# Row indices spread ahead of the gates' softmax, evictions between one-hots, keys and last modulation blocks by the Pool queue, four more blocks preloaded

## The chip, the cores and the metric

One core of one Trainium2 chip runs the whole kernel. The metric is the device time of one execution in microseconds (us); lower is better. The engines are TensorE (PE, with its weight loads PEld), VectorE (DVE), ScalarE (ACT), GpSimd (POOL) and SyncE (SP). Each works through its own queue in order. A DMA is issued from the queue of SP, ACT or POOL, and lands later.

## What is computed

One layer of a decoder for 256 tokens of width 1024: a token mixer, then PEER, a layer that picks for each token 128 of 16384 one-neuron experts. The change lies in PEER and in the modulation that its result is scaled by:

```python
mod = cs @ w_ada[l] + b_ada[l]              # six columns; the last, gt_f, scales PEER's result
q = (xt @ w_q).reshape(n, 8, 2, 128)
s = einsum('nhpd,phkd->nhpk', q, sub_keys)  # scores against two key tables of 128 per head
s1, i1 = top_k(s[:, :, 0], 16)
s2, i2 = top_k(s[:, :, 1], 16)
comb = s1[..., :, None] + s2[..., None, :]  # 256 candidates
top_s, pos = top_k(comb, 16)
experts = cand[pos]                         # cand = i1 * 128 + i2
gate = softmax(top_s)
a = gelu(einsum('nd,nhkd->nhk', xt, u_tab[experts]))
y = einsum('nhk,nhkd->nd', gate * a, v_tab[experts])
x = rmsnorm(x + gt_f * y)
```

## The kernel before

**Stages.** The mixer runs until about 274 us. Then come the queries (PE tile pq): 16 blocks of w_pq, each split by ACT (L98, tile hi) and DVE (L99, tile lo) into two parts, three products of eight matmuls each. `query` scales a block on DVE (L1174) and adds a bias on ACT (L1177). Between them stand the scores of token half 1 (`score`, PE tile psc) against the table `keys`, which SP loads at L1190. Then PEER's tables follow, dense: 128 blocks of `u` (PE tile pu, 16 instructions per block; "the u half"), ACT's gelu into the array W (`gelu`, every second block), and 128 blocks of `v` (PE tile Y, "the Y half"), which contract W. W lies in the tile GB, block by block. A table block is 512 KB; `table_ahead` (L746 to L754) issues it into a ring of ten tiles (tags raw and hl), from SP, one in five from ACT.

**Two ways for the tokens.** The last 96 tokens (SPARSE = 64 and 32) are not in the dense products (DT = 160 columns). For them POOL gathers the rows of the chosen experts by an indirect DMA of 128 rows of 4 KB, 512 KB (L1055): 96 gathers from u, 96 from v. DVE multiplies each u row with the token (L1076, a sum per row) and adds each v row, scaled, into `hrow` (L1085, L1087). The generator `sparse` holds four buffers and keeps three gathers ahead. Its indices come from the array `pairs`, which `spread` (L1036) writes from `own`, the indices and gates of token half 1, by six small DMAs from POOL. At the end PE folds hrow into Y (L1280) and the last sums, transposes and the output follow.

**From scores to one-hots.** `topk(tt)` runs on DVE for half 1, then for half 0: rounds of max, index and replace over eight heads, the combination, and the selection `sel` (L1004). Then it subtracts the maximum (L1008), ACT applies Exp (L1009), DVE normalises (L1012 to L1015), writes `own` (L1018, L1020), calls `spread`, and PE transposes indices and gates (tile pidx). `g_phase` works on chunks of 8 of the 160 dense tokens. Per chunk: DVE makes the one-hot `oe` (L1119) and scales it by the gate's high part `gth` into ob[:, 0] (L1121); ACT makes `od` with 8 instructions (L1125) and `oa` (L1129), and scales oe by the low part `gtl` into ob[:, 1] with 8 instructions (L1131); PE multiplies oa and ob (tile pG, 16 matmuls); and the result is evicted into W, by DVE for the blocks that already have their gelu (L1111, `kd` of 128) and by ACT for the others (L1113). Y needs all of W.

**What sets the order.** From the queries on the program order is written out. In the loop over u blocks `spend(work, more)` takes from the generators topk and g_phase as much as a budget allows: each `yield` names its cost, a block brings BU = 2.1. Once `n_first` is set, `due` grows by RATE = 0.75 per block, and each whole unit emits one gather product of `sparse` (and the gather that reuses its buffer) and takes 1.27 from the budget. In the Y half it is one per block. `ada_col(5)` sums the eight blocks of the last modulation column on DVE (L165): four in the stage before the queries, four among them (L1192), loaded by SP into the same four raw buffers as w_pq.

The lines that set the pace in the u half:

```python
        more = BU
        if n_first[0]:
            due[0] += RATE
            while due[0] >= 1:
                due[0] -= 1
                advance(rows)
                more -= 1.27
        if n_gated[0] and k % 2:
            more -= 0.45
        spend(work, more)
```

## Time and profile before

| | |
|---|---|
| time, three runs | median 980.07 us (977.72 to 986.09) |
| the profiled execution | 983.35 us, its span 981.6 us |
| PE | 919.2 us busy, 94% |
| DVE, ACT, POOL | 628.6, 356.3, 205.5 us busy |
| mean granted PE clock | 0.959 of full speed |
| DMA | 306.43 MB, 312 GB/s in the mean |
| queues | SP (q1) 179.39 MB, POOL (q0) 100.77 MB, ACT (q10) 25.17 MB |

The profile is one execution. In rows of windows the columns are: the stretch, its length, the busy time of PE, PEld, DVE, ACT and POOL (with the count of instructions), then PEclk, the granted clock as a share of 2.4 GHz (0.50 is 1.2 GHz), the busy share of the DMA engines and GB/s. A wait is put down to what ended it. Matmuls are pipelined: each fp32 matmul is two instructions here, and the pace is read from one start to the next.

### The profile page before, as it was taken

The page shows a single profiled execution, that of the slowest core. Times are in us where ns is not written, and L with a number is a line of the kernel's source. Part 1 is how long each engine was busy: PE and PEld are TensorE (multiplying, and loading weights), DVE is VectorE, ACT ScalarE, POOL GpSimd, SP SyncE. Part 2 cuts the span into 40 slices and gives each one's busy share as a digit, 9 for nine tenths or more (in the row PEclk, how much of TensorE's full clock was granted, in tenths as well). Part 3 has the DMA queues.
Part 4 walks back from the last instruction along what each step waited for, and adds up shares of the span by engine and source line. Part 5 has one row for each costly group of instructions (what it writes and reads, how often), then busy time and mean ns, then how long its engine had stood idle before and what let it go on. Part 6 is the DMA issues. An engine that isn't in the chain of part 4 may idle for free.

```text
span 981.6 us, 17461 instructions
## 1 busy us (share of the span) xinstructions
PE 919.2 (94%) x6794; PEld 886.5 (90%) x6794; DVE 628.6 (64%) x1373; ACT 356.3 (36%) x856; POOL 205.5 (21%) x212
## 2 busy tenths in 40 slices
PE   6999999999997999999979999989999999999926
PEld 5899887789987999999978999989999999999925
DVE  7898748866986791678875777654444444444463
ACT  4474348755545422101159998920000000000002
POOL 1000000000000001333433324333333333333340
PEclk8999869999997999999989999999999999999967
DMA  9888434356676487999998999979999999999981
GB/s 355 318 274 259 149 117 162 108 172 215 205 234 248 158 295 226 385 418 419 419 387 319 352 358 354 356 303 419 418 419 419 418 419 418 418 420 418 416 279 44
DMA packets 85810, 306.43 MB, mean 312 GB/s; under 512 B 9601, under 2 KB 10049, under 8 KB 85601
## 3 DMA queue, kind: packets, MB, share of 16 engines
q1 hardware_dynamic: 50976, 179.39, 49.4%
q0 software_dynamic: 27840, 100.77, 26.3%
q10 hardware_dynamic: 6912, 25.17, 6.7%
q8 instruction: 53, 0.87, 0.4%
q14 instruction: 29, 0.23, 0.1%
HBM read 304.14 MB, written 1.05 MB: 311 GB/s over the span
## 4 chain that ended last, share of the span: by engine, by line
PE 41%; DMA 33%; DVE 9%; issue 7%; ACT 6%; POOL 3%; DVEq 0%; ACTq 0%; POOLq 0%; SPq 0%
DMA gat<-in_v_row_dram,pairs 22%; PE pu L117 11%; DMA gat<-in_u_row_dram,pairs 8%; PE col L117 8%; PE pq L117 4%; POOL gat L1055 3%; DVE hrow L1087 3%; PE row L117 3%; PE pbr L117 2%; ACT od L1125 2%; ACT ob L1131 2%; PE po L117 2%; PE pout L117 1%; PE pS L117 1%; PE ph L117 1%
## 5 line engine op out<-in xcount | busy, mean ns | idle before, releaser
L117 PE MATMUL pu<-h,tab 128*128 128x160 f32 x2048 | 289.7, 302 | 5.4 <-ACT gb L1160 5.4
L117 PEld LDWEIGHTS pu<-h,tab 128*128 128x128 f32 x2048 | 283.3, 192 | 5.7 <-ACT gb L1160 5.7
L117 PE MATMUL Y<-gb,tab 128*128 128x160 f32 x2048 | 282.7, 300 | 1.3 <-DMA tab<-in_v_row_dram 0.8
L117 PEld LDWEIGHTS Y<-gb,tab 128*128 128x128 f32 x2048 | 279.8, 191 | 2.8 <-DMA tab<-in_v_row_dram 2.7
L1087 DVE SCALAR_TENSOR_TENSOR hrow<-gat,act,hrow 128x1024 f32<-128x1024 f32 x94 | 120.8, 1285 | 132.9 <-DMA gat<-in_v_row_dram,pairs 132.9
L1076 DVE SCALAR_TENSOR_TENSOR gat<-gat,hrow 128x1024 f32<-128x1024 f32 x96 | 116.4, 1221 | 53.1 <-DMA gat<-in_u_row_dram,pairs 52.5
L1055 POOL DMA_INDIRECT gat<-in_u_row_dram,pairs x96 | 105.1, 1095 | 195.4 <-DVE gat L1076 149.0
L1055 POOL DMA_INDIRECT gat<-in_v_row_dram,pairs x96 | 92.1, 959 | 171.7 <-DVE hrow L1087 149.1
L99 DVE TENSOR_TENSOR lo<-raw,hi 128x1024 fp32r<-128x1024 f32 (+2 forms) x67 | 80.5, 1207 | 24.5 <-ACT hi L98 24.1
L1302 ACT ACTIVATE gb<-gb 128x256 f32<-128x256 f32 x8 | 3.3, 417 | 224.2 <-DVE gb L1300 224.2
L98 ACT CAST hi<-raw 128x1024 fp32r<-128x1024 f32 (+2 forms) x67 | 69.1, 1038 | 43.1 <-PE pq L117 8.8
L1160 ACT ACTIVATE gb<-pu 128x320 f32<-128x320 f32 (+18 forms) x60 | 22.8, 382 | 114.7 <-PE pu L117 105.7
L165 DVE SCALAR_TENSOR_TENSOR raw<-raw,crow 128x1024 f32<-128x1024 f32 x48 | 58.2, 1220 | 9.8 <-DMA raw<-in_ada_t_dram 9.7
L1125 ACT ACTIVATE od<-iota,n1T 128x128 f16<-128x128 f16 x160 | 49.7, 439 | 0.0
L1131 ACT ACTIVATE ob<-oe,gtl 128x128 f16<-128x128 f16 x160 | 49.5, 429 | 0.0
L1111 DVE SCALAR_TENSOR_TENSOR gb<-pG,gb 128x480 f32<-128x480 f32 (+18 forms) x40 | 20.7, 557 | 38.5 <-PE pG L117 29.8
L117 PE MATMUL col<-hlo,hi 128*128 128x256 f32 x160 | 40.8, 289 | 0.0
L117 PE MATMUL col<-hh,hi 128*128 128x256 f32 x160 | 40.3, 286 | 0.0
L117 PE MATMUL pq<-hx,hi 128*128 128x258 f32 x128 | 33.4, 301 | 1.9 <-ACT gb L1176 1.9
L117 PE MATMUL col<-xr,wf 128*128 128x256 f32 x128 | 30.5, 404 | 4.3 <-ACT xr L271 4.3
L117 PEld LDWEIGHTS col<-xr,wf 128*128 128x128 f32 x128 | 26.1, 205 | 8.8 <-ACT xr L271 4.7
L904 POOL IOTA gb<- 128x16 f16 x1 | 0.1, 150 | 156.3 <-DVE r L192 156.3
(336 smaller groups left out, 1294.5 us busy)
## 6 DMA issues: line engine op xcount, KB each, us to landing
tab<-in_u_dram SPq DMA_DIRECT2D x105, 512.0 KB
tab<-in_v_row_dram SPq DMA_DIRECT2D x103, 512.0 KB
raw<-in_ada_t_dram SPq DMA_DIRECT2D x48, 512.0 KB
tab<-in_v_row_dram ACTq DMA_DIRECT2D x25, 512.0 KB
tab<-in_u_dram ACTq DMA_DIRECT2D x23, 512.0 KB
raw<-in_w_col_dram SPq DMA_DIRECT2D x20, 512.0 KB
raw<-in_w_pq_dram SPq DMA_DIRECT2D x16, 512.0 KB
raw<-in_w_row_dram SPq DMA_DIRECT2D x12, 512.0 KB
```

Of the source, the lines that this page charges most:

```text
L98: nc.scalar.copy(hi, src)
L99: trail = lambda: nc.vector.tensor_tensor(lo, src, hi.bitcast(F32), op=OP.subtract)
L117: nc.tensor.matmul(out, l, r, start=start, stop=stop, skip_group_check=True)
L165: nc.vector.scalar_tensor_tensor(r, r, 1.0, crow, op0=OP.mult, op1=OP.mult, accum_out=mod[:, k, j:j + 1])
L1055: nc.gpsimd.indirect_dma_start(out=r, out_offset=None, in_=A[table], in_offset=bass.IndirectOffsetOnAxis(ap=pairs[:, 0, j:j + 1].bitcast(U ...
L1076: nc.vector.scalar_tensor_tensor(r, r, 1.0, hrow[group_of[j]], op0=OP.mult, op1=OP.mult, accum_out=act[:, 0, j:j + 1])
L1087: nc.vector.scalar_tensor_tensor(acc, r, act[:, 1, j:j + 1], acc, op0=OP.mult, op1=OP.add)
L1111: nc.vector.scalar_tensor_tensor(w, g[:, :kd], 1.0 / GS, w, op0=OP.mult, op1=OP.mult)
L1125: nc.scalar.activation(od[:, t // 2, :, t % 2], iota[:, :, 0], AF.Abs, bias=n1T[:, c * TC + t:c * TC + t + 1])
L1131: nc.scalar.activation(ob[:, 1, t // 2, :, t % 2], oe[:, t // 2, :, t % 2], AF.Copy, scale=gtl[:, c * TC + t:c * TC + t + 1])
L1160: nc.scalar.activation(W[:, k:k + 2, nd:], o[:, :, nd:], AF.Gelu_apprx_tanh)
L1302: nc.scalar.activation(sq[:, j], x2[:, j], AF.Square)
```

## The change

1. `topk` writes the row indices into `own` as soon as `sel` is there, and sets `n_first`; the normalising part becomes a generator of its own, `gates(tt)`. For half 1 it runs after four pieces of `topk(0)`. `spread(what, groups)` sends indices and gates apart: the indices of the first 64 tokens, three gathers, the other indices; the gates when they are there. After that `due` is set to -5 x RATE.
2. In `g_phase` the one-hots of chunk c stand ahead of the eviction of chunk c-2, and that ahead of the product of chunk c-1. `gtl` becomes fp16, and DVE scales oe by it in one instruction instead of ACT in eight. `oe` has one buffer instead of two.
3. `keys` is loaded from the POOL queue right after the pool of the PEER stage opens; the eight blocks of the last modulation column come by the POOL queue into the tiles of tags oa and ob (four buffers), and DVE sums them all among the queries (3 <= j < 11).
4. The first four blocks of `u` are loaded by SP among the last loads of w_pq into the part of GB that W fills later; the ring of ten begins with block 4. So 14 blocks are on the way before the u half, instead of 10.

```diff
-    def ada_col(k, ahead=0):
+    def ada_col(k, room=None):
+        r = []
         for j in range(ND):
-            if ahead and j + ahead < ND:
-                r.append(load(A["ada_t"][k, j + ahead]))
-            ada_sum(k, j, r[j] if ahead else None)
+            while room and len(r) < min(j + 4, ND):
+                r.append(room(len(r)))
+                nc.gpsimd.dma_start(r[-1], A["ada_t"][k, len(r) - 1])
+            ada_sum(k, j, r[j] if room else None)
             yield
...
     own_room(1)
+    nc.gpsimd.dma_start(keys, A["keys"])
...
-    gtl = pe.tile([P, T], F32, name="gtl")
+    gtl = pe.tile([P, T], F16, name="gtl")
...
+        if tt == NT - 1:
+            nc.vector.scalar_tensor_tensor(own[:, 0].bitcast(U32), sel[:, 1], float(P), sel[:, 0], op0=OP.mult,
+                                           op1=OP.add)
+            n_first[0] = 1
         g = g.rearrange("p (h k) -> p h k", h=8)
         nc.vector.tensor_tensor(g, top, top[:, :, 0:1].to_broadcast([P, 8, 16]), op=OP.subtract)
         nc.scalar.activation(g, g, AF.Exp)
-        yield 0.2
-        yield 1.4
+        yield 0.5
+
+    def gates(tt):
...
         if tt == NT - 1:
-            nc.vector.scalar_tensor_tensor(own[:, 0].bitcast(U32), sel[:, 1], float(P), sel[:, 0], op0=OP.mult,
-                                           op1=OP.add)
             nc.vector.tensor_copy(own[:, 1], g.rearrange("p h k -> p (h k)"))
-            spread()
-            n_first[0] = 1
+            spread(1)
...
+        spread(0, [0])
         for i in range(AHEAD_G):
             get()
+        spread(0, range(1, len(SPARSE)))
+        yield 0.0
...
+                nc.vector.tensor_tensor(ob[:, 1], oe, tok(gtl, c, P), op=OP.mult)
...
-                for t in range(TC):
-                    nc.scalar.activation(ob[:, 1, t // 2, :, t % 2], oe[:, t // 2, :, t % 2], AF.Copy,
-                                         scale=gtl[:, c * TC + t:c * TC + t + 1])
...
-        if j == 4:
-            nc.sync.dma_start(keys, A["keys"])
-        if 2 <= j < 7:
+        if j == 2:
+            ada_end = ada_col(5, lambda i: pe.tile([P, WMAX], F32, name="ada5", tag=("oa", "ob")[i % 2], bufs=2))
+        if 2 < j < 12:
             advance(ada_end)
+        if 6 < j < 11:
+            r = GB[:, (j - 7) * WMAX:(j - 6) * WMAX]
+            nc.sync.dma_start(r, tabs[j - 7])
+            held.append(r)
...
-            work = chain(topk(1), topk(0), g_phase())
+            first = topk(0)
+            work = chain(topk(1), islice(first, 4), gates(1), first, gates(0), g_phase())
...
         if n_first[0]:
+            if n_first[0] == 1:
+                n_first[0] = 2
+                advance(rows)
+                due[0] = -WAIT * RATE
             due[0] += RATE
```

**What stands where: DVE, the end of `topk(1)`.** Of before, from the last sum of the selection (L1004) to the first gather product (L1076); gb is the tile that holds the working arrays.

```order
L1004 TENSOR_TENSOR gb<-gb 128x128
L1008 TENSOR_TENSOR gb<-gb 128x128
L1012 TENSOR_REDUCE gb<-gb 128x8
L1013 RECIPROCAL gb<-gb 128x8
L1014 TENSOR_SCALAR gb<-gb 128x8
L1015 TENSOR_TENSOR gb<-gb 128x128
L1018 SCALAR_TENSOR_TENSOR own<-gb 128x128
L1020 COPY own<-gb 128x128
L1076 SCALAR_TENSOR_TENSOR gat,act<-gat,hrow_3014 128x1024
L1033 TENSOR_TENSOR gtl<-pidx,gth 128x128
```

Of the change, from the same sum (now L1007):

```order
L1007 TENSOR_TENSOR gb<-gb 128x128
L1010 SCALAR_TENSOR_TENSOR own<-gb 128x128
L1015 TENSOR_TENSOR gb<-gb 128x128
L942 MAX gb<-gb 128x8 x2
L944 MAX_INDEX gb<-gb 128x8 x2
L946 MATCH_REPLACE gb<-gb 128x128 x2
L949 MAX gb<-gb 128x8 x2
L951 MAX_INDEX gb<-gb 128x8 x2
```

The write of the indices (own, 128x128 from gb) has moved ahead of the subtraction and of everything that waits for ACT's Exp; two heads of `topk(0)` and then the normalising part (L1022 to L1028) follow it.

**POOL, from the last work of the mixer (kTs) to the gathers.** Of before:

```order
L407 MEMSET kTs 128x512
L902 IOTA iota 128x256
L904 IOTA gb 128x16
L1041 DMA pairs<-own 64x2x64 x2
L1041 DMA pairs<-own 32x2x32 x4
L1055 DMA gat<-in_u_row_dram,pairs 128x1024 x96
L1055 DMA gat<-in_v_row_dram,pairs 128x1024 x96
```

Of the change (the tiles ada_... are the buffers of the modulation blocks; eight such rows stand there, the last is shown):

```order
L894 DMA gb<-in_keys_dram 128x2048
L901 IOTA iota 128x256
L903 IOTA gb 128x16
L173 DMA ada_3076<-in_ada_t_dram 128x1024
```

```order
L173 DMA ada_3244<-in_ada_t_dram 128x1024
L1049 DMA pairs<-own 64x64 x2
L1064 DMA gat<-in_u_row_dram,pairs 128x1024 x3
L1049 DMA pairs<-own 32x32 x4
L1049 DMA pairs<-own 64x64 x2
L1049 DMA pairs<-own 32x32 x4
L1064 DMA gat<-in_u_row_dram,pairs 128x1024 x93
L1064 DMA gat<-in_v_row_dram,pairs 128x1024 x96
```

Nine large loads now stand on this queue ahead of the spread, and the spread is 12 small DMAs in two parts around the first three gathers; the fourth gather stands behind the gates' part.

**DVE, the end of the u half.** Of before, the last evictions of pG (L1111) and the products that apply a late gelu (L1158):

```order
L1111 SCALAR_TENSOR_TENSOR gb<-pG,gb 128x120x4 x4
L1158 TENSOR_TENSOR gb<-gl,gb 128x2x144
L1076 SCALAR_TENSOR_TENSOR gat,act<-gat,hrow_3015 128x1024 x2
L1158 TENSOR_TENSOR gb<-gl,gb 128x320
L1076 SCALAR_TENSOR_TENSOR gat,act<-gat,hrow_3015 128x1024
```

Of the change:

```order
L1123 TENSOR_TENSOR oe<-iota,i2T 128x1024
L1125 TENSOR_TENSOR ob<-oe,gth 128x1024
L1088 SCALAR_TENSOR_TENSOR gat,act<-gat,hrow_3002 128x1024
L1167 TENSOR_TENSOR gb<-gl,gb 128x2x136
L1088 SCALAR_TENSOR_TENSOR gat,act<-gat,hrow_3002 128x1024
L1127 TENSOR_TENSOR ob<-oe,gtl 128x1024
L1139 SCALAR_TENSOR_TENSOR gb<-pG,gb 128x128x4 x6
L1167 TENSOR_TENSOR gb<-gl,gb 128x2x136
L1088 SCALAR_TENSOR_TENSOR gat,act<-gat,hrow_3002 128x1024 x18
```

The evictions of the last three chunks (x6, over all 128 blocks) stand together behind the last block, where before the last two chunks were evicted over 120 blocks and four gelu pairs followed.

## Rows read from the trace of the kernel before

**Rows 1.** PE waits, whole span: waiter <- awaited: us in total, times, longest us.

```profile
PE Y L117 <- DVE hrow L1087: 22.2, 1, 22.2
PE psc L117 <- DMA gb<-in_keys_dram: 7.7, 1, 7.7
PE pG L117 <- ACT gb L1113: 7.0, 5, 3.5
PE pu L117 <- ACT gb L1160: 5.4, 1, 5.4
...
PE pq L117 <- ACT gb L1176: 1.9, 1, 1.9
```

**Rows 2.** Windows by stage: us, busy us of each engine, PEclk, DMA share, GB/s.

```profile
396.00:480.00 84.00, 84.00 (x621) 84.00 (x620) 65.98 (x264) 8.31 (x19) 26.41 (x29) 1.00 1.02 414
...
520.00:640.00 120.00, 114.70 (x991) 113.32 (x990) 82.27 (x155) 115.52 (x376) 39.97 (x34) 1.00 0.95 349
...
700.00:930.00 230.00, 228.72 (x1674) 227.18 (x1673) 103.27 (x84) 1.77 (x3) 76.08 (x81) 1.00 1.03 419
930.00:960.00 30.00, 7.84 (x62) 7.70 (x60) 19.85 (x16) 0.00 (x0) 13.18 (x12) 0.70 0.76 262
```

**Rows 3.** The chain of waits, in order of time: start us, us, what.

```profile
293.79 7.99 DMA gb<-in_keys_dram
...
303.90 4.36 PE pq L117 x24
308.26 0.22 PE psc L117 x2
308.49 2.90 PE pq L117 x24
...
377.11 4.36 PE pu L117 x32
...
959.74 5.92 PE Y L117 x24
```

**Rows 4.** Windows of the query stage, columns as above.

```profile
285.00:290.00 5.00, 3.12 (x26) 2.92 (x25) 2.91 (x8) 2.57 (x7) 0.15 (x1) 1.00 0.37 123
...
300.00:305.00 5.00, 3.18 (x15) 3.18 (x16) 3.06 (x5) 2.06 (x5) 0.00 (x0) 0.50 0.97 387
```

**Rows 5.** Instructions on tile pu: min/median/max ns, first and last start us.

```profile
L117 PE MATMUL pu<-h,tab x2048: 299/299/636, 336.6 to 658.7; 128*128 128x160 f32 x187
```

**Rows 6.** PE in order of time, one chunk: start us, us, instruction.

```profile
510.00 1.08 PE L117 MATMUL pG<-ob,oa 128*128 128x128 f16 x16
510.92 1.30 PE L117 MATMUL pu<-h,tab 128*128 128x160 f32 x8
```

**Rows 7.** ACT in order of time: Exp of half 0, with its wait.

```profile
493.75 0.31 ACT L1009 ACTIVATE gb<-gb 128x128 f32<-128x128 f32 x1 [10.16 <-DVE gb L1008]
```

**Rows 8.** POOL in order of time: rank iota, spread, first gather.

```profile
287.48 0.15 POOL L904 IOTA gb<- 128x16 f16 x1 [156.34 <-DVE r L192]
385.30 3.58 POOL L1041 DMA_DIRECT2D pairs<-own  x6 [97.67 <-DVE own L1020]
391.37 1.03 POOL L1055 DMA_INDIRECT gat<-in_u_row_dram,pairs  x1 [2.49 <-PE pu L117]
```

**Rows 9.** DVE in order of time: after the selection of token half 1.

```profile
383.58 0.29 DVE L1012 TENSOR_REDUCE gb<-gb 128x8 f32<-128x128 f32 x1 [12.95 <-ACT gb L1009]
...
397.95 1.23 DVE L1076 SCALAR_TENSOR_TENSOR gat<-gat,hrow 128x1024 f32<-128x1024 f32 x1 [12.97 <-DMA gat<-in_u_row_dram,pairs]
```

**Rows 10.** The page, part 5: the ACT instructions that scale one-hots by gtl.

```profile
L1131 ACT ACTIVATE ob<-oe,gtl 128x128 f16<-128x128 f16 x160 | 49.5, 429 | 0.0
```

**Rows 11.** DVE groups, 380:660 us: count, busy, mean ns, idle before.

```profile
L1076 DVE SCALAR_TENSOR_TENSOR gat<-gat,hrow 128x1024 f32<-128x1024 f32 x82 | 99.3, 1220 | 30.9 <-DMA gat<-in_u_row_dram,pairs 30.4 <-issue 0.4
L1121 DVE TENSOR_TENSOR ob<-oe,gth 128x1024 f16<-128x1024 f16 x20 | 13.8, 692 | 0.7
...
L1111 DVE SCALAR_TENSOR_TENSOR gb<-pG,gb 128x480 f32<-128x480 f32 x4 | 2.5, 655 | 5.3 <-PE pG L117 5.2
```

More of the change, by code (lines that the diff above doesn't have):

```diff
@@ L1 @@
 from contextlib import ExitStack, nullcontext
-from itertools import chain
+from itertools import chain, islice
 import numpy as np
@@ L51 @@
 Q_SPARE = 1.0
+WAIT = 5
 TC = 8
@@ L165, in ada_sum @@
         nc.vector.scalar_tensor_tensor(r, r, 1.0, crow, op0=OP.mult, op1=OP.mult, accum_out=mod[:, k, j:j + 1])
-    def ada_col(k, ahead=0):
-        r = [load(A["ada_t"][k, j]) for j in range(ahead)]
-        if ahead:
-            yield
+    def ada_col(k, room=None):
+        r = []
         for j in range(ND):
-            if ahead and j + ahead < ND:
-                r.append(load(A["ada_t"][k, j + ahead]))
-            ada_sum(k, j, r[j] if ahead else None)
+            while room and len(r) < min(j + 4, ND):
+                r.append(room(len(r)))
+                nc.gpsimd.dma_start(r[-1], A["ada_t"][k, len(r) - 1])
+            ada_sum(k, j, r[j] if room else None)
             yield
@@ L750, in table_ahead @@
             return
-        tag = "raw" if i % 5 in (0, 3) or i < 3 else "hl"
+        tag = "raw" if (i - 4) % 10 in (0, 1, 2, 6) else "hl"
         r = stream.tile([P, WMAX], F32, name="tab", tag=tag, bufs=4 if tag == "raw" else HL)
-        (nc.scalar if i >= 16 and i % 5 == 1 else nc.sync).dma_start(r, tabs[i])
+        (nc.scalar if i >= 20 and i % 5 == 1 else nc.sync).dma_start(r, tabs[i])
         held.append(r)
@@ L922, in hybrid_block @@
     sco = {}
+    n_scored = [0, 0]
     def score(tt, hp, bank):
@@ L953, in topk @@
     def topk(tt):
+        assert n_scored[tt] == 16 or tt == 1
         sc_ = sco[tt]
@@ L1034, in topk, with spread @@
         yield 0.3
-    def spread():
-        for i, n in enumerate(SPARSE):
+    def spread(what, groups=range(len(SPARSE))):
+        for i in groups:
+            n = SPARSE[i]
             t = t_of[i] - (T - P)
             for g in range(P // n):
-                nc.gpsimd.dma_start(pairs[g * n:g * n + n, :, j_of[i]:j_of[i] + n], own[t:t + n, :, g * n:g * n + n])
+                nc.gpsimd.dma_start(pairs[g * n:g * n + n, what, j_of[i]:j_of[i] + n],
+                                    own[t:t + n, what, g * n:g * n + n])
     gat = []
@@ L1103, in g_phase @@
         for c in range(n + 2):
+            if c < n:
+                od = pe.tile([P, TC // 2, P, 2], F16, name="od", bufs=1)
+                for t in range(TC):
+                    nc.scalar.activation(od[:, t // 2, :, t % 2], iota[:, :, 0], AF.Abs,
+                                         bias=n1T[:, c * TC + t:c * TC + t + 1])
+                oe = pe.tile([P, TC // 2, P, 2], F16, name="oe", bufs=1)
+                nc.vector.tensor_tensor(oe, io, tok(i2T, c, P), op=OP.is_equal)
+                ob = pe.tile([P, 2, TC // 2, P, 2], F16, name="ob", bufs=2)
+                nc.vector.tensor_tensor(ob[:, 0], oe, tok(gth, c, P), op=OP.mult)
+                yield 1.4
+                nc.vector.tensor_tensor(ob[:, 1], oe, tok(gtl, c, P), op=OP.mult)
+                oa = pe.tile([P, TC // 2, P, 2], F16, name="oa", bufs=2)
+                nc.scalar.activation(oa, od, AF.Relu, scale=-1.0, bias=ones[:, 0:1])
+                ab[c] = (oa, ob)
+                yield 0.7
             if c > 1:
@@ L1115, in g_phase @@
                 yield 0.5 + 0.005 * kd
-            if c < n:
-                oe = pe.tile([P, TC // 2, P, 2], F16, name="oe", bufs=2)
-                nc.vector.tensor_tensor(oe, io, tok(i2T, c, P), op=OP.is_equal)
-                ob = pe.tile([P, 2, TC // 2, P, 2], F16, name="ob", bufs=2)
-                nc.vector.tensor_tensor(ob[:, 0], oe, tok(gth, c, P), op=OP.mult)
-                yield 1.0
-                od = pe.tile([P, TC // 2, P, 2], F16, name="od", bufs=1)
-                for t in range(TC):
-                    nc.scalar.activation(od[:, t // 2, :, t % 2], iota[:, :, 0], AF.Abs,
-                                         bias=n1T[:, c * TC + t:c * TC + t + 1])
-                yield 0.4
-                oa = pe.tile([P, TC // 2, P, 2], F16, name="oa", bufs=2)
-                nc.scalar.activation(oa, od, AF.Relu, scale=-1.0, bias=ones[:, 0:1])
-                for t in range(TC):
-                    nc.scalar.activation(ob[:, 1, t // 2, :, t % 2], oe[:, t // 2, :, t % 2], AF.Copy,
-                                         scale=gtl[:, c * TC + t:c * TC + t + 1])
-                ab[c] = (oa, ob)
-                yield 0.0
             if 0 < c <= n:
@@ L1206, in hybrid_block @@
             nc.scalar.activation(h2[:, k], h2[:, k], AF.Identity, scale=modA[:, 1, k:k + 1], bias=mod[:, 3, k:k + 1])
-    while len(held) < 10:
+    while len(held) < 14:
         table_ahead()
@@ L1218, in hybrid_block @@
             mm(o[:, k % 2], r[:, dt * P:(dt + 1) * P], h2[:, dt, :DT], dt == 0, dt == ND - 1)
-        table_ahead()
+        if k > 3:
+            table_ahead()
         if k % 2:
```

10 lines of the change are left out of this document (6 added, 4 removed).

## The prediction, made before the result was known

> **What bounds the kernel now.** I read the waits of the TensorE (PE) first, since the PE is busy for most of the span, then the chain of waits, then the stages by windows. The reader is to see four places where PE time is lost, and one resource under them.
>
> At the end, the dense second half (tile Y) has run out of work and PE stands 22.2 us until the last gathered row has been added by the DVE [rows 1]. So the last thing to finish is the gather stream, and the DMA is why: 414 to 419 GB/s from 396 to 480 and from 700 to 930 us, falling to 349 between 520 and 640 [rows 2]. A 512 KB transfer (0.524 MB, a table block or a gather alike) takes 1.25 us at 419 GB/s. PE eats one table block in 2.18 us (two blocks, 32 instructions, in 4.36 us [rows 3]), which is 240 GB/s; the 179 GB/s left are one gather in 2.93 us.
>
> The other three places lie before the Y half. The query stage waits 7.7 us for the key table and 1.9 us for an eviction [rows 1], and after the long wait the granted clock is 0.50 [rows 4]: eight scores take from 301.8 to 303.9 us instead of 0.9 (two take 0.22), the next query block 4.36 instead of 2.90 us [rows 3]. That is 7.7 + 1.9 + 1.2 + 1.5 = 12.3 us. After the 1.9 us pause the clock stayed at 1.00 [rows 4]. The u half runs from 336.6 to 658.8 us (its last instruction starts at 658.7), 322.2 us [rows 5]. Its work is 128 blocks of 2.18 (279.0), 17 score pairs of 0.22 (3.7), 20 one-hot chunks (pG) of 0.92 from start to next start [rows 6] (18.4) and 22 transposes of 0.11 (2.4): 303.5 us. The excess of 18.7 us is the wait for the gelu evictions (5.4), those of pG (7.0) [rows 1] and slow clock behind them. The first has a cause upstream: ACT stands 10.2 us before the softmax's Exp for a DVE subtraction [rows 7], which is queued behind products that wait for gathers. The second is ACT itself: 115.5 of 120 us busy from 520 to 640 [rows 2].
>
> **The change part by part.**
>
> *Keys and last modulation blocks on the Pool queue.* Before, the keys leave SP at 293.8 and need 8.0 us behind other loads [rows 3]. Now they are the Pool queue's first transfer in this stage, behind the tile release that the rank iota waited for, 287.5 us [rows 8]; with the same 8.0 us they land at 295.5, and since the loads of w_pq no longer share their four buffers with modulation blocks, the chain up to that release should be shorter. PE is ready at 294.1. What can be lost: all eight modulation products now stand in the DVE's queue between query evictions, the first behind a transfer issued after the keys; a late one holds the evictions, so the score matmuls. Bounds: none of the 12.3 us comes back, or all. I take 8.3, one late block (about 4 us) still showing, because the keys' row is the nearest. The modulation products themselves (eight of the DVE's 1.2 us kind) lie under 2.90 us of PE for each query block.
>
> *Four more blocks preloaded.* The ring is ten tiles deep either way, so by the time Y begins as many bytes have come in; costed at nothing. It costs no PE time because the blocks come during the queries, where the DMA has room (123 GB/s at 285 to 290 us [rows 4]). Bounds 0 and a gain of 4 x 1.25 = 5 us.
>
> *Row indices ahead of the softmax.* DVE has the selected indices at 370.6 and then waits 12.95 us for Exp [rows 9]; the Pool issues the spread at 385.3 and the first gather at 391.4 [rows 8], and the first product starts at 398.0 [rows 9]. Without Exp on that path and with the query stage 8 us shorter, the first three gathers leave 23 us earlier, at about 368 (362.3 plus the 6.1 us from spread to gather). But the first product is placed 5 blocks after that (counted through the emission loop: block 25, was 21), and the fourth gather now stands on the Pool queue behind the gates' spread. So the stream starts no earlier against PE; it starts with its buffers full, three gathers or about 9 us ahead. That is what the Exp of the other token half needs: it came 10.2 us late and now sits at block 60 instead of 64. I count that wait as gone.
>
> *Chunks.* 160 ACT instructions (49.5 us [rows 10]) become 20 DVE products like those of ob with gth, 0.692 us [rows 11], 13.8 us. ACT falls from 96% to about 60% of the stage. DVE has room: 82.3 of 120 us [rows 2]. Moving the evictions behind the one-hots adds no instruction, but the emission loop costs a chunk dearer, so the last three chunks (17, 18, 19) are evicted at block 127, where before all ended at block 120. Six evictions of 0.655 us [rows 11] then follow each other on DVE, 3.9 us, with two pG groups (already counted) inside: PE stands some 3 to 5 us before Y. Of the 18.7 us I leave 8: 4 at this boundary and 4 for evictions that DVE brings late. Gain 10.7; bounds 0 and 15.
>
> *What is left for Y.* By 660 us 82 of 192 gathers were used [rows 11]; now 78 are, by the order of the loop. Four more at the end cost 1.25 us each while table blocks still come, or 2.0 us each in the last stretch (262 GB/s [rows 2]): 5 to 8; less what has landed in the buffers meanwhile. I take 5. The remainder of Y takes what it took: 658.8 to 959.7 us, then 21.9 us of tail from 959.7 [rows 3] to the span's end.
> Bytes can be checked against this: 110 gathers and about 118 table blocks are 119.5 MB, 285 us at the 419 GB/s of [rows 2], of 300.9 us taken. The Trainium skill, "SBUF — State Buffer" (Summary: rules for kernel authors), says to estimate transfers from HBM at about 358 GB/s. By it these bytes alone would need an estimated 334 us and the sum below would come out 33 us higher; the trace moves them faster, so the measurement decides.
>
> **Sum.** 981.6 - 8.3 - 10.7 + 5 = 967.6 us of span. The profiled execution took 983.35 us, 1.75 us around its span; the median of the runs, 980.07, is 3.3 us below it. So 967.6 + 1.75 - 3.3 = 966 us.
>
> **Rivals.**
> *The Pool queue brings nothing earlier.* Keys and modulation blocks arrive late enough that PE waits as long as before, and only the u half gains: 966 + 8.3 = 974. For it: the keys cannot start before 287.5, and the DVE stands in order behind every block. Against: a gather of the same 512 KB takes the Pool 1.03 us to issue while DVE works [rows 8].
> The Trainium skill, "SBUF — State Buffer" (Who interferes with whom), warns that transfers issued from GpSimd wait for descriptors while DVE runs copies or casts in a two-port mode, and advises the SP or ACT queue instead; it exempts two-input products, which fill the DVE here. No run here shows such a wait; that warning is this rival.
>
> *The end does not follow.* The four extra gathers cost 2.93 us each, 11.7 instead of 5, and half of the u gain (5.4) stays as DVE lateness: 966 + 6.7 + 5.4 = 978. For it: DVE is what everything is now queued on. Against: DVE's 69%.
>
> *Slower.* The gather stream falls behind the loop in the u half, and since the chunk evictions and the one-hots' third product stand behind gather products on the DVE, PE waits for it at the boundary. Each gather of lag costs 2.93 us once. Beyond 13.8 / 2.93, about 5 gathers, the gain is gone; at 9 it is 966 + 26 = 992. For it: a lag of 10.2 us (three to four gathers) stands in the trace before Exp [rows 7]. Against: 30.9 us of DVE waits for gathers over the whole u half [rows 11], and a slower PE block in the chunk stage (2.18 + 0.92 per three blocks) that asks less of the DMA.
>
> *Every wait goes.* The 4 us in the query stage and 4 in the u half vanish: 958.
>
> **How the numbers follow.** Chances: forecast 0.62 (its own range 959 to 973), Pool queue 0.12, the end does not follow 0.11, slower 0.06, every wait gone 0.09. The range reaches from 955 (below 958, should preloading bring its bound) to 979. About 1% is what a measurement of this kernel can tell from no change; 1% below 980 is 970. Faster takes the forecast without its upper edge (0.56) and the case of 958: 0.65. Within 1% are that edge, 974 and 978: 0.29. Slower: 0.06.
>
> **What would show it.** Right: the wait for the keys under 3 us and no 0.50 clock in the query stage; pu starting at about 328; first gather at about 368; Exp of the first token half without a wait of DVE; ACT under 70% in the chunk stage; a new PE wait of some 4 us for a pG eviction just before Y; Y starting near 640; and still 25 us or so of PE standing for the last gather. Wrong: a wait of the DVE for modulation blocks beyond 5 us, Y starting after 648, or the end following Y's start by much more than 328 us.

## The result

Over five rounds the changed kernel takes 969.38 us in the median (967.31 to 972.93), the kernel before beside it 981.52: a ratio of 0.9877, with a 95% interval of 0.9838 to 0.9916. That is 1.2% faster; 966 us had been predicted, with a range of 955 to 979. The profiled execution, the fastest of the five, took 967.31 us, its span 965.5.

The waits of PE after (waiter <- awaited: us in total, times, longest):

```profile
PE Y L118 <- DVE hrow L1099: 25.2, 1, 25.2
...
PE psc L118 <- ACT gb L1186: 3.9, 2, 3.6
PE pG L118 <- ACT gb L1141: 3.6, 2, 1.8
...
PE pG L118 <- DVE gb L1139: 1.5, 2, 1.3
...
PE Y L118 <- DVE gb L1139: 0.8, 1, 0.8
```

Against [rows 1], the waits for the key table (7.7 us) and of the query block (1.9) are gone, one of 3.6 us before the scores has come; the gelu wait (5.4) is gone, the pG waits on ACT fell from 7.0 to 3.6, and two short waits (1.3 and 0.8 us) stand at the boundary to Y. The wait for the last gathered row has grown from 22.2 to 25.2 us.

Windows after (the stretch, its length, busy us of PE, PEld, DVE, ACT, POOL, then PEclk, DMA share, GB/s):

```profile
290.00:295.00 5.00, 1.37 (x12) 1.18 (x11) 3.38 (x6) 1.15 (x3) 0.53 (x1) 1.00 1.02 418
295.00:300.00 5.00, 5.00 (x31) 5.00 (x30) 5.00 (x9) 3.05 (x6) 0.95 (x2) 0.66 0.94 353
...
500.00:600.00 100.00, 96.37 (x807) 95.63 (x806) 69.00 (x135) 54.30 (x162) 37.58 (x29) 1.00 0.96 359
600.00:640.00 40.00, 37.71 (x327) 36.79 (x327) 32.77 (x59) 18.88 (x60) 14.80 (x12) 1.00 0.98 375
...
915.00:943.00 28.00, 2.91 (x25) 2.77 (x23) 19.92 (x16) 0.00 (x0) 14.22 (x12) 0.58 0.77 255
```

The DMA is full in a part of the query stage (418 GB/s from 290 to 295), has room in the chunk stage (359 and 375), and at the end moves gathers alone while PE stands. ACT is at 54% in the chunk stage; before it stood at 96% [rows 2].

Tiles pu and Y (x count: min/median/max ns, first and last start), for the stage lengths:

```profile
L118 PE MATMUL pu<-h,gb x64: 299/299/302, 328.3 to 337.8; 128*128 128x160 f32 x64
...
L118 PE MATMUL Y<-gb,tab x2048: 299/299/614, 639.0 to 955.9; 128*128 128x160 f32 x187
```

So pu starts at 328.3 and Y at 639.0 us. For all kernels of this study the span is cut at four places: the first query matmul, the first on pu, the first on Y, the end of the last gathered product. The first three lengths follow, in us (one profiled execution each), with PE's stand for the last gather, the median time and its ratio to the kernel before:

| kernel | query to pu | pu to Y | Y to last gather | PE's stand | median | ratio, 95% |
|---|---|---|---|---|---|---|
| before | 62.7 | 322.2 | 300.8 | 22.2 | 980.3 to 981.5 | |
| changed | 56.0 | 310.7 | 304.0 | 25.2 | 969.38 | 0.9877 (0.9838 to 0.9916) |
| keys_by_sp | 56.0 | 310.7 | 304.2 | 25.2 | 967.72 | 0.9882 (0.9846 to 0.9917) |
| ada_by_sp | 56.0 | 310.7 | 304.1 | 25.3 | 968.45 | 0.9855 (0.9830 to 0.9881) |
| ada_later | 53.9 | 310.7 | 304.9 | 25.5 | 965.88 | 0.9832 (0.9805 to 0.9859) |
| preload_10 | 56.7 | 310.7 | 304.4 | 25.1 | 967.51 | 0.9864 (0.9826 to 0.9902) |
| idx_with_gates | 56.0 | 319.4 | 304.8 | 25.3 | 976.71 | 0.9966 (0.9942 to 0.9991) |
| gtl_by_act | 56.2 | 332.2 | 304.2 | 25.2 | 988.87 | 1.0088 (1.0055 to 1.0122) |
| evict_first | 56.3 | 308.2 | 304.8 | 24.2 | 966.55 | 0.9858 (0.9831 to 0.9886) |
| gtl_act_evict_first | 55.7 | 309.6 | 305.9 | 24.7 | 970.19 | 0.9895 (0.9856 to 0.9935) |
| rate95 | 56.8 | 311.0 | 282.0 | 3.5 | 947.91 | 0.9657 (0.9634 to 0.9680) |
| before_rate95 | 62.7 | 320.8 | 283.2 | 3.1 | 963.07 | 0.9816 (0.9775 to 0.9858) |
| best95 | 53.3 | 307.1 | 283.3 | 3.8 | 939.16 | 0.9579 (0.9540 to 0.9618) |
| best100 | 53.1 | 315.4 | 279.1 | none | 941.60 | 0.9605 (0.9569 to 0.9642) |

The stage lengths repeat within about 1 us; what lies ahead of the first query matmul does not (it starts between 268.7 and 275.7 us). So a stage is judged by its length, the whole by the ratio.

### The profile page after: what moved, and what is told of

Read it like the earlier page. It is cut to its first block, busy times and chain, and to the rows that moved or that the text cites. A ratio compares the mean times of both kernels' runs of the same rounds, so it can differ in the third digit from the quotient of the medians.

```text
span 965.5 us, 17340 instructions
## 1 busy us (share of the span) xinstructions
PE 913.3 (95%) x6794; PEld 880.4 (91%) x6794; DVE 639.4 (66%) x1394; ACT 312.6 (32%) x695; POOL 221.5 (23%) x227
## 4 chain that ended last, share of the span: by engine, by line
PE 57%; DMA 23%; issue 9%; DVE 5%; POOL 4%; ACT 1%; DVEq 0%; POOLq 0%; ACTq 0%; SPq 0%
PE pu L118 24%; DMA gat<-in_v_row_dram,pairs 21%; PE col L118 9%; POOL gat L1064 4%; PE pq L118 4%; PE row L118 3%; DVE hrow L1099 3%; PE pout L118 2%; PE pbr L118 2%; PE po L118 2%; PE pS L118 1%; PE pkv L676 1%; PE pG L118 1%; PE ph L118 1%; PE Y L118 1%
## 5 line engine op out<-in xcount | busy, mean ns | idle before, releaser
L118 PE MATMUL pu<-h,tab 128*128 128x160 f32 x1984 | 275.9, 299 | 0.0
L118 PEld LDWEIGHTS pu<-h,tab 128*128 128x128 f32 x1984 | 270.5, 190 | 0.0
L1064 POOL DMA_INDIRECT gat<-in_u_row_dram,pairs x96 | 112.6, 1172 | 188.8 <-DVE gat L1088 154.8
L1169 ACT ACTIVATE gb<-pu 128x320 f32<-128x320 f32 (+14 forms) x64 | 24.3, 379 | 110.8 <-PE pu L118 101.5
L166 DVE SCALAR_TENSOR_TENSOR raw<-raw,crow 128x1024 f32<-128x1024 f32 x40 | 48.7, 1220 | 7.0 <-DMA raw<-in_ada_t_dram 6.9
L1139 DVE SCALAR_TENSOR_TENSOR gb<-pG,gb 128x512 f32<-128x512 f32 (+17 forms) x40 | 21.3, 574 | 16.9 <-ACT gb L1169 16.5
L118 PEld LDWEIGHTS col<-hh,hi 128*128 128x128 f32 x160 | 30.1, 188 | 2.5 <-issue 2.4
```

The lines of the kernel that those rows point to most:

```text
L118: nc.tensor.matmul(out, l, r, start=start, stop=stop, skip_group_check=True)
L166: nc.vector.scalar_tensor_tensor(r, r, 1.0, crow, op0=OP.mult, op1=OP.mult, accum_out=mod[:, k, j:j + 1])
L1064: nc.gpsimd.indirect_dma_start(out=r, out_offset=None, in_=A[table], in_offset=bass.IndirectOffsetOnAxis(ap=pairs[:, 0, j:j + 1].bitcast(U ...
L1139: nc.vector.scalar_tensor_tensor(w, g[:, :kd], 1.0 / GS, w, op0=OP.mult, op1=OP.mult)
L1169: nc.scalar.activation(W[:, k:k + 2, nd:], o[:, :, nd:], AF.Gelu_apprx_tanh)
```

## The experiments

**Keys back on SP, modulation blocks on the Pool queue** (keys_by_sp).

```diff
-    nc.gpsimd.dma_start(keys, A["keys"])
+        if j == 4:
+            nc.sync.dma_start(keys, A["keys"])
```

> The changed kernel, but the key table is issued by SP inside the loop over the query blocks (at j = 4) as before; the modulation blocks stay on the Pool queue. Theory (a late key table costs PE time in the query stage, and everything behind it moves with it): PE waits 5 to 8 us for the keys again, a slow stretch of the clock stands behind the wait, tile pu starts at 334 to 338 us instead of 328.3, and the end moves by the same 6 to 10 us. Rival 1 (the gather stream is bound by the DMA and takes up the difference): pu starts later, but the end moves by under 3 us. Rival 2 (the modulation blocks on the Pool queue did it, the keys would come in time by SP too): pu within 2 us of 328.3 and no end difference.

Nothing changed: 56.0 us from the first query matmul to pu. SP's queue shows why (start us, us, instruction):

```profile
279.19 0.33 SPq L1198 DMA_DIRECT2D gb<-in_keys_dram  x1
```

SP issues the keys 10.5 us after the first query matmul (268.7); in the kernel before it was at 293.79 [rows 3], 19.8 us after (274.0). SP then no longer stands for buffers that modulation blocks occupy. Rival 2 holds: the Pool queue is not needed for the keys.

**Modulation blocks back on SP, keys on the Pool queue** (ada_by_sp). `ada_col` is the one of before, its eight blocks loaded by SP into the buffers of w_pq.

```diff
...
-        if j == 2:
-            ada_end = ada_col(5, lambda i: pe.tile([P, WMAX], F32, name="ada5", tag=("oa", "ob")[i % 2], bufs=2))
-        if 2 < j < 12:
+        if 2 <= j < 7:
             advance(ada_end)
```

> The changed kernel with the keys on the Pool queue, but the eight last modulation blocks are loaded by SP into the four buffers that the loads of w_pq use, as before the change. With the keys by SP and the modulation blocks by the Pool, the run keys_by_sp had the same query stage as the changed kernel, so the theory is now that the shared buffers were the cause: SP's loads of w_pq (and, before, the keys behind them) waited for buffers that DVE's modulation products held. It expects the pauses of the query stage back: PE standing 4 to 10 us in sum between 280 and 310 us (3.6 in the changed kernel), tile pu starting 3 to 9 us later in step with that, and the end moving by the same. Rival (the keys alone on a queue of their own are enough, either way out of SP's order will do): PE stands under 4 us there and neither pu nor the end moves by more than 2 us.

Again nothing was lost: 56.0 us, with pauses of 3.1 us in sum. So the theory after the first run, that the shared buffers were the one cause, falls too. Here the keys leave the Pool in time although the loads of w_pq and modulation wait for each other as before (the same row's end names what the queue stood for):

```profile
288.62 0.72 POOL L898 DMA_DIRECT2D gb<-in_keys_dram  x1 [284.93 <-ACT gb L1189]
```

They land at 293.9 us; the first pause for scores is one of 0.47 us at 296.9. What costs the 7.7 us is the keys standing in SP's queue behind loads that wait for buffers that modulation blocks hold; taking either out of that queue ends it. The two moves are alternatives, and their gain of 6.7 us (62.7 to 56.0) is not a sum.

**The first modulation product one query block later** (ada_later).

```diff
-        if 2 < j < 12:
+        if 3 < j < 13:
             advance(ada_end)
```

> The changed kernel with each product of the last modulation blocks one query block later (3 < j < 13 instead of 2 < j < 12), so that DVE asks for the first block about 3 us later; nothing else is moved. Theory (the pause of 3.6 us before the first scores is DVE waiting 3.8 us for that first block, with the query eviction queued behind it): the pause is under 1 us, no slow stretch of the clock behind it, pu starts 3 to 5 us earlier and the end is 3 to 5 us earlier. Rival 1 (the pause is the keys themselves or the loads of w_pq, which come no earlier): the pause stays at 3 us or more. Rival 2 (the end is set by the gather stream): pause gone, end moves by less than 1 us.

In the changed kernel DVE stands for the first block, and the query eviction is behind it:

```profile
291.62 1.22 DVE L166 SCALAR_TENSOR_TENSOR ada<-ada,crow 128x1024 f32<-128x1024 f32 x1 [3.83 <-DMA ada<-in_ada_t_dram]
```

One block later the pause is 1.1 us, followed by three of 0.4 to 0.7, 2.7 us in sum:

```profile
295.00:300.00 5.00, 3.93 (x33) 3.72 (x32) 4.08 (x6) 2.30 (x5) 0.53 (x1) 1.00 1.02 412
300.00:305.00 5.00, 4.61 (x38) 4.40 (x38) 5.00 (x10) 2.71 (x7) 1.06 (x2) 1.00 1.03 419
```

The granted clock stays at 1.00, and the stage is 2.1 us shorter (53.9). The cause is shown; the size was below the 3 to 5 us expected, since the DMA is full there (412 and 419 GB/s) and the blocks are late once more. The whole time moved by less than its interval.

**Ten blocks preloaded** (preload_10): the four loads into GB left out, and a load for every block used.

> The changed kernel without the four blocks preloaded into the keys' tile: ten blocks are held ahead of the u half, and every block's use starts another load. Theory (behind the fourth block both kernels hold ten blocks ahead, so the four are worth nothing): pu start, Y start and end within 2 us of the changed kernel. Rival (bytes brought in ahead are bytes that the DMA need not move later, 4 x 1.25 us): the end 4 to 6 us later.

All lengths within 0.7 us of the changed kernel, the ratio the same (0.9864 and 0.9877): the four blocks bring nothing.

**Indices with the gates** (idx_with_gates): in `topk` the write of `own` and `n_first` goes back behind the normalising, WAIT is 0.

```diff
...
             nc.vector.tensor_copy(own[:, 1], g.rearrange("p h k -> p (h k)"))
             spread(1)
+            n_first[0] = 1
```

> The changed kernel, but row indices and gates are spread together, behind the gates' softmax; the first gathered product stays at the same place in the loop (block 25). Theory (the early indices fill the buffers ahead of the stream, and a stream that starts 2 to 3 gathers short keeps DVE late until the chunk stage): first gather at about 380 us instead of 366, DVE late by 6 to 9 us at the Exp of the other token half, PE standing 3 to 6 us there for gelu evictions, tile Y starting at 642 to 646 instead of 639, and the end 3 to 7 us later. Rival (the loop's lag is taken up before anything waits for it): Y start and end within 1.5 us of the changed kernel.

Y starts 9.5 us later, the stretch from pu to Y is 8.7 us longer, and the ratio goes back from 0.9877 to 0.9966. The first three gathers leave the Pool at 386 instead of 366 us:

```profile
386.08 1.02 POOL L1062 DMA_INDIRECT gat<-in_u_row_dram,pairs  x1 [4.24 <-DMA pairs<-own]
```

PE then waits at eight places, 12.4 us in sum, between 474 and 649 us (waits of PE):

```profile
PE pG L118 <- ACT gb L1139: 6.7, 4, 1.9
...
PE pidx L1032 <- DVE gb L1020: 1.9, 1, 1.9
PE pG L118 <- ACT oa L1127: 1.6, 1, 1.6
PE pG L118 <- DVE gb L1137: 1.3, 1, 1.3
```

In the changed kernel they are five, 5.9 us. The end is later, a little above the expected 3 to 7 us, but the loss is only in part where the theory puts it. At the Exp of the other token half DVE is 2.9 us late and PE waits 1.9 us, for the gates that it transposes (pidx) and not for a gelu; the lower clock around it costs an estimated 1.6 us ((1 - 0.84) x 10):

```profile
474.93 0.31 ACT L1011 ACTIVATE gb<-gb 128x128 f32<-128x128 f32 x1 [2.87 <-DVE gb L1010]
```

```profile
470.00:480.00 10.00, 8.10 (x49) 7.86 (x48) 6.18 (x15) 6.59 (x16) 2.86 (x4) 0.84 1.03 420
```

Ahead of the four waits for ACT's evictions (6.7 us) DVE is not late: it stands 3.4, 3.0, 3.0 and 4.0 us until ACT has made the gelu of a pair of blocks that PE has only just ended, and PE's product of the next chunk stands right behind that pair. The first of them, on three engines in order of time:

```profile
490.02 6.74 PE L118 MATMUL pu<-h,tab 128*128 128x160 f32 x48
497.17 0.44 ACT L1167 ACTIVATE gb<-pu 128x320 f32<-128x320 f32 x1 [2.22 <-PE pu L118]
497.64 0.82 DVE L1137 SCALAR_TENSOR_TENSOR gb<-pG,gb 128x288 f32<-128x288 f32 x2 [3.42 <-ACT gb L1167]
498.13 0.72 ACT L1139 ACTIVATE gb<-pG 128x224 f32<-128x224 f32 x2 [0.52 <-DVE gb L1137]
498.54 1.08 PE L118 MATMUL pG<-ob,oa 128*128 128x128 f16 x16 [1.78 <-ACT gb L1139]
```

Undoing this edit also moves the chunk products among the u blocks, since the loop places them by its budget: in PE's order 72 and 79 blocks stand ahead of the second and the fourth chunk's product, 71 and 77 in the changed kernel. So 8.7 us is what the edit is worth with the order that the loop then makes; what the early gathers are worth alone is not shown.

**The third product back on ACT** (gtl_by_act).

```diff
-                nc.vector.tensor_tensor(ob[:, 1], oe, tok(gtl, c, P), op=OP.mult)
...
+                for t in range(TC):
+                    nc.scalar.activation(ob[:, 1, t // 2, :, t % 2], oe[:, t // 2, :, t % 2], AF.Copy,
+                                         scale=gtl[:, c * TC + t:c * TC + t + 1])
```

> The changed kernel, but the third product of the one-hots (oe with gtl) is made again by eight ACT instructions for each chunk instead of one DVE product; the order of one-hots and evictions stays the new one. Theory (ACT was what held the chunks): ACT over 85% busy between 500 and 600 us (54% in the changed kernel), PE waits for pG and gelu evictions back at 6 to 10 us in sum, tile Y starting at 645 to 650 instead of 639, and the end later by the same 6 to 10 us. Rival 1 (the gather stream sets the end, a slower u half leaves the DMA more room): Y start later, but the end by under 3 us. Rival 2 (the new order of evictions brought the gain, not the product): Y start within 2 us of 639.

It cost 21.5 us from pu to Y, twice the most expected, and not by the load that the theory names: ACT is 70% busy. The waits for ACT's evictions are 13.1 us longer (16.7 to 3.6); most of the rest goes with the lower clock behind them (0.93 from 500 to 600, 1.00 in the changed kernel).

```profile
PE pG L118 <- ACT gb L1143: 16.7, 7, 5.2
```

```profile
500.00:600.00 100.00, 89.33 (x701) 88.13 (x701) 54.39 (x107) 70.23 (x224) 28.57 (x25) 0.93 0.83 307
```

One of the seven pauses, on three engines in order of time, ACT first:

```profile
486.31 2.47 ACT L1120 ACTIVATE od<-iota,n1T 128x128 f16<-128x128 f16 x8
488.82 1.15 ACT L1128 ACTIVATE oa<-od,ones 128x1024 f16<-128x1024 f16 x1
489.87 2.46 ACT L1130 ACTIVATE ob<-oe,gtl 128x128 f16<-128x128 f16 x8
492.21 0.41 ACT L1171 ACTIVATE gb<-pu 128x320 f32<-128x320 f32 x1
493.14 0.72 ACT L1143 ACTIVATE gb<-pG 128x232 f32<-128x232 f32 x2 [0.52 <-DVE gb L1141]
```

```profile
492.65 0.81 DVE L1141 SCALAR_TENSOR_TENSOR gb<-pG,gb 128x280 f32<-128x280 f32 x2 [6.80 <-ACT gb L1171]
```

```profile
483.81 4.56 PE L118 MATMUL pu<-h,tab 128*128 128x160 f32 x32
493.55 1.70 PE L118 MATMUL pG<-ob,oa 128*128 128x128 f16 x16 [5.18 <-ACT gb L1143]
```

The gelu of two blocks (L1171) could run once PE has ended them, at 488.4 us at the latest; it starts at 492.2, behind nine one-hot instructions of the next chunk. DVE's eviction of pG waits for it (6.8 us idle), ACT's eviction for that, and PE for the bank.

**Evictions first** (evict_first): the block of evictions ahead of the one-hots, as before, the product still on DVE.

```diff
         for c in range(n + 2):
+            if c > 1:
...
             if c < n:
```

> The changed kernel with a chunk's evictions ahead of the next chunk's one-hots again, as before the change; the third product stays on DVE. Theory (the relief of ACT is the product's, the order of evictions only moves waits): Y start and end within 3 us of the changed kernel, the pauses for pG of 1.8 us may change place. Rival 1 (the new order brought part of the gain): Y starts 4 to 8 us later and so does the end. Rival 2 (the old order is now the better one, because fewer chunks are left over at the boundary to Y): the pauses before Y shrink from 2.1 us and the end is 1 to 3 us earlier.

The old order is the better one by 2.5 us in the stage (308.2); by the whole time the two can't be told apart. The pauses of 1.8 us are gone; at the boundary 3.2 us are waited for the one-hot oa instead of 1.3.

**Both undone** (gtl_act_evict_first).

> The changed kernel with both parts of the chunk edit undone: evictions ahead of the one-hots, and the third product by eight ACT instructions. Measured so far, from pu's first matmul to Y's first: 310.7 us (changed kernel), 308.2 (evictions first, product on DVE), 332.2 (new order, product on ACT). Theory (where ACT is the bound, its place in ACT's queue decides how long an eviction waits: behind one-hot work in the new order, ahead of it in the old): this stretch takes 313 to 319 us, and the time lies between that of the changed kernel and 8 us above it. Rival (the eight ACT instructions cost about 20 us in either order): 326 us or more, the time about 16 to 22 us above the changed kernel.

```profile
PE pG L118 <- ACT oa L1140: 3.2, 1, 3.2
```

```profile
500.00:600.00 100.00, 100.00 (x844) 99.52 (x843) 66.79 (x129) 83.82 (x273) 37.01 (x30) 1.00 0.98 373
```

The stretch takes 309.6 us, below the theory's range, and as long as in the changed kernel (310.7). ACT is busier than in gtl_by_act (84% to 70%), yet PE does not wait for it between 500 and 600. With the indices early, the order of evictions and the product's engine together are worth nothing: either order goes with the product on DVE, only the old one with it on ACT. In each order the chunk products stand at the same blocks with the product on either engine, so the pairs compare cleanly: the product on ACT costs 21.5 us with the one-hots first and 1.4 us (309.6 to 308.2) with the evictions first.

**More gathers in the chunk stage** (rate95). No part of the change is undone; the step goes at the bound that all kernels above share, PE's stand of 22 to 25 us.

```diff
+RC = 0.95
...
-        more = BU
+        more = BU + (RC - RATE) * 1.27 if n_gated[0] else BU
...
-            due[0] += RATE
+            due[0] += RC if n_gated[0] else RATE
```

> The changed kernel with more gathered products in the chunk stage: 0.95 a block there instead of 0.75 (and the loop's allowance for the chunks raised by the same DVE time, 0.25 us a block), so that 89 instead of 78 of 192 gathers are used when Y begins. Theory (the end is set by the gather stream, and the DMA had room between 500 and 640 us, 359 to 375 of 419 GB/s): the DMA moves 395 to 415 GB/s there, Y starts within 4 us of 639, PE stands 8 to 14 us for the last gather instead of 25.2, and the end is 9 to 16 us earlier. Rival 1 (the DMA or DVE is not as free as the mean says: blocks or products come late in the chunk stage): Y starts 6 us later or more and the end moves by under 4 us. Rival 2 (the end is not the gather stream's): PE's stand at the end shrinks but the end moves by under 2 us.

```profile
PE Y L119 <- DVE hrow L1100: 3.5, 1, 3.5
```

```profile
500.00:600.00 100.00, 97.01 (x819) 96.06 (x819) 80.27 (x151) 53.75 (x163) 41.01 (x37) 1.00 1.00 400
600.00:640.00 40.00, 37.35 (x323) 36.20 (x321) 35.34 (x63) 20.20 (x61) 14.74 (x15) 1.00 1.02 414
```

Y starts at 640.1 us, 1 us later, the DMA is filled, and from Y's start to the last gathered product it takes 22.0 us less: 11 gathers at 2.0 us. The median is 21 us below the changed kernel's. The gain was above the 9 to 16 us expected because each gather is worth what it costs in the last stretch.

**The same step on the kernel before** (before_rate95).

> The kernel before, with nothing changed but the rate of gathered products in the chunk stage: 0.95 a block instead of 0.75 (91 instead of 82 used when Y begins), with the loop's allowance raised by the same DVE time. In the changed kernel the same step was worth about 20 us. Theory (the kernel before is also bound by the gather stream at its end, 22.2 us of PE standing, and the DMA has room in its chunk stage at 349 GB/s): Y starts 0 to 8 us later, since ACT is 96% busy there and DVE is late already, PE stands 3 to 8 us at the end, and the time is 8 to 18 us below that of the kernel before. Rival (without the relief of ACT the higher rate only makes the chunk stage longer): Y starts 12 us later or more, the gain is under 4 us.

17 us of gain (0.9816), with all waits of the query stage and of ACT left in (waits of PE):

```profile
PE pG L118 <- ACT gb L1114: 8.1, 5, 3.2
PE psc L118 <- DMA gb<-in_keys_dram: 5.5, 1, 5.5
...
PE Y L118 <- DVE hrow L1088: 3.1, 1, 3.1
```

Ten more gathers before Y, 17.6 us less behind its start, 1.8 us for each. They are ten and not nine because the expectation's 82 has one of the Y half in it: in the kernel before, Y starts at 658.8 us and the 82nd product behind it, after 81:

```profile
659.93 1.22 DVE L1076 SCALAR_TENSOR_TENSOR gat<-gat,hrow 128x1024 f32<-128x1024 f32 x1
```

By the medians this one number does more than the whole change (17 and 12 us); the intervals of the two ratios still overlap a little (0.9775 to 0.9858 and 0.9838 to 0.9916). The rival's doubt about ACT falls: the stretch from pu to Y is no longer than before (320.8 and 322.2 us).

**Together** (best95: rate95, evict_first and ada_later; best100 the same with 1.0).

> The changed kernel with three steps together: evictions ahead of the one-hots (308.2 instead of 310.7 us from pu to Y), the last modulation products one query block later (53.9 instead of 56.0 us from the first query matmul to pu), and 0.95 gathered products a block in the chunk stage. Theory (the steps stand at different places and add): about 4 us below rate95, so 942 to 946 us. Rival (what is gained ahead of Y returns as PE's stand at the end, since the gather stream is again the last): within 1.5 us of rate95's 948, the stand at the end 5 to 8 us instead of 3.5.

> As best95, with 1.0 gathered product a block in the chunk stage (92 used when Y begins instead of 89). Theory (after rate95 the end is PE's, with 3.5 us left to gain): PE's stand at the end under 1 us, Y starts at most 3 us later because the DMA then has no room left in the chunk stage; the time within 3 us of best95. Rival 1 (the stream still bounds): 3 us or more below best95. Rival 2 (the DMA is over its limit in the chunk stage, DVE falls behind and PE waits for chunks): 3 us or more above best95.

best95 takes 939.16 us, 4.2% below the kernel before and about 3% below the changed one; the gains add (53.3, 307.1, and a stand of 3.8 us), to a little more than the 942 to 946 us expected. With 1.0 the stand is gone and the stretch ahead of Y is 8.3 us longer, where at most 3 were expected; about half of that are waits at the boundary (7.0 us instead of 3.0), the rest three shorter pauses and a lower clock (0.92 from 600 to 640):

```profile
PE pG L119 <- DVE gb L1124: 4.5, 1, 4.5
...
PE pG L119 <- ACT gb L1126: 2.4, 2, 1.7
```

The times of the two differ by less than their intervals; by PE's stand (3.8 us and none), the rate at which the gather stream and PE end together should lie between them, which was not run.

## Why the prediction was right, and where its reasons were not

**Query stage, -8.3.** From the first query matmul to pu it was -6.7; the other 1.6 us of the earlier pu lie ahead of the stage, where runs differ anyway, so that pu starts at the predicted 328 is luck by that much. What is left there is 5.6 of the 12.3 us: pauses of 3.9, as foretold one late modulation block with the evictions behind it, and the slower clock behind them (0.66 from 295 to 300). Wrong was the reading that the keys' place on the Pool queue brings this: keys_by_sp and ada_by_sp show that either move does. "No 0.50 clock" held only for a whole window: a mean of 0.66 over 5 us says that the lower level (0.50) was granted for 3.4 of them.

The rival that the Pool queue brings nothing earlier did not come. The Pool issued each block in about half a microsecond, also from 295 to 305 us, where DVE is busy without a break with two-input products:

```profile
285.82 2.17 POOL L173 DMA_DIRECT2D ada<-in_ada_t_dram  x4
...
299.57 0.53 POOL L173 DMA_DIRECT2D ada<-in_ada_t_dram  x1 [2.69 <-DVE ada L166]
```

The Trainium skill, "SBUF — State Buffer" (Who interferes with whom), warns of transfers from GpSimd that wait for descriptors, and exempts such products; the trace agrees for these products, and no run here was made to test the warning itself.

**Preload, 0.** Right: behind the fourth block both hold ten ahead, and preload_10 has the same lengths without the four. The reason given for the query stage did not last, though: the DMA had room there before (123 GB/s), but moves 418 and 353 GB/s from 290 to 300 us after the change.

**Row indices.** Right in place and in effect: the first gather leaves at 366.0 us (368 predicted), the first product starts as long after pu's start as before (61.5 and 61.4 us) but no longer waits for its gather, and Exp of half 0 no longer waits:

```profile
365.99 1.03 POOL L1064 DMA_INDIRECT gat<-in_u_row_dram,pairs  x1 [2.18 <-DMA pairs<-own]
```

```profile
389.76 1.21 DVE L1088 SCALAR_TENSOR_TENSOR gat<-gat,hrow 128x1024 f32<-128x1024 f32 x1
```

```profile
466.56 0.31 ACT L1016 ACTIVATE gb<-gb 128x128 f32<-128x128 f32 x1
```

**Chunks, -10.7.** The stretch from pu to Y fell by 11.5 us and its excess over the prediction's work is 7.2 us (8 predicted): waits of 5.9 us (3.6 for evictions, 2.3 at the boundary), and 1.3 us of work that the sum of 303.5 us lacks, since PE is busy for 304.8 us. The granted clock is 1.00 throughout (from 500 to 640 above). Of the 18.7 us before, then, 12.8 were waits (7.0, 5.4 and one of 0.4), 1.3 were work, and the remaining 4.6 go with the lower clock around the long pauses, which these rows show before the change:

```profile
480.00:500.00 20.00, 14.59 (x92) 14.35 (x92) 17.58 (x32) 4.08 (x6) 9.51 (x8) 0.87 1.03 419
500.00:520.00 20.00, 18.97 (x152) 18.70 (x152) 13.72 (x28) 16.83 (x52) 7.22 (x7) 0.96 0.97 359
...
640.00:660.00 20.00, 18.99 (x137) 18.99 (x137) 10.52 (x20) 3.19 (x12) 7.12 (x6) 0.91 0.74 279
```

The gain is thus 6.9 us of waits and 4.6 us of clock. The sum is right, the cause is not. The step that failed is "The second is ACT itself: 115.5 of 120 us busy from 520 to 640". With ACT's old work and the old order back, but early indices, PE does not wait for ACT in the chunk stage until the boundary; with late indices and ACT relieved, it waits 6.7 us for ACT's evictions of pG. The 96% were read as a bound; what the two pauses shown above (gtl_by_act, idx_with_gates) have in common is an eviction that waits for a gelu, behind one-hots in the one, behind PE's own last blocks in the other. Of the 11.5 us, 8.7 go with the edit of the indices, in part by lateness at Exp and in part by where the chunk steps then stand. One piece stays open: the changed code also names other costs for its chunk steps and so spreads the 20 chunks over more blocks. gtl_act_evict_first keeps these costs, and the old ones were not tried alone, so how much of the gain is placing, which the prediction does not count, is not known.

**What is left for Y, +5.** From Y's start to the end it was 3.7 us more: 3.2 to the last product, the rest in the tail. For a gather moved ahead of Y, rate95 and before_rate95 measure 2.0 and 1.8 us (22.0 / 11, 17.6 / 10), near the upper of the two prices in the sum. Its count was off by one: 81 were used when Y began, not 82, so three fewer now, not four. Three came to 3.2 us, about 1.1 us each and nearer to the lower price; the sum had allowed for what lands in the buffers meanwhile, which no run measures alone.

**Sum and rivals.** In the profiles -1.6 - 6.7 - 11.5 + 3.7 = -16.1 us (981.6 to 965.5); in the medians -12.1, since the kernel before was profiled in an execution 1.8 us above its median and the changed one in its fastest, 2.1 us below. So the forecast's 966 us, which takes 3.3 us off for the first and nothing for the second, lies 3.4 us under the median, while its span of 967.6 lies 2.1 us over the one profiled. The rival "Slower" sets lag against a gain of 13.8 us; the sum's own is 14.0. "The end does not follow" did not come: end and Y start moved together within 3.7 us. Nor did the gathers fall behind: PE's last wait before Y is 0.8 us. Rightly seen, and not used by the change, was the first paragraph's bound: the gather stream ends last, while the DMA has room in the chunk stage.

## What to carry to other kernels

Two fixes of one wait can be alternatives: undo them one at a time before adding up their gains. An engine's busy share does not tell whether it is waited for (ACT at 84% cost nothing, at 70% it cost 16.7 us of PE); what stands ahead of the awaited instruction in its queue does. Undoing an edit in a loop that places its steps by a budget moves other steps as well: compare the orders before the difference is called the edit's. And where the profile shows a resource full at the end with room for the same work earlier, move that work first: here one pacing number was worth 17 to 21 us, the four edits 12.

## What the runs showed of the hardware

After a pause of 2.49 us of PE (ada_by_sp) the granted clock was 0.70 in the next window, so it stood at the lower level (1.2 of 2.4 GHz) for part of it; after one of 1.88 us in the kernel before it had stayed at 1.00, and after pauses of 1.1 us and less in ada_later as well. In idx_with_gates a pause of 1.91 us comes with 0.84 (470 to 480), so the length of a pause alone does not tell these cases apart. The rows of ada_by_sp:

```profile
285.00:290.00 5.00, 2.51 (x19) 2.30 (x19) 3.04 (x7) 1.98 (x4) 1.38 (x2) 0.96 0.39 124
290.00:295.00 5.00, 5.00 (x33) 5.00 (x32) 4.87 (x6) 2.27 (x6) 1.01 (x2) 0.70 0.91 340
```

By these shares the lower level cost an estimated 1.7 us in ada_by_sp (0.04 x 5 + 0.30 x 5) and as much in the changed kernel (0.34 x 5). The two take the same 56.0 us though ada_by_sp pauses 0.8 us less (3.1 and 3.9 us); that lies within what stage lengths differ by.
